# A projection stage written out by ticks of 24 matmuls, with convolution taps over about 1024 tokens

## The chip, the cores and the metric

The kernel runs on one core of one Trainium2 chip. The metric is the device time of one execution, in microseconds (us); of several runs the median counts. Engines are named as in the profile: PE is the matmul engine (PEld its weight loads), DVE the vector engine, ACT the scalar engine, POOL the GpSimd engine, SP the engine whose queue issues most DMA transfers. "L159" is line 159 of the kernel before.

## What is computed

An encoder layer is applied with the same weights to two requests, of 2048 and of 1024 tokens, all in float32. Cut to what matters:

```python
h = x @ w_in + b_in                       # 1024 -> 5632 features
glu_a, glu_b, conv_gate, q, k, v, attn_gate, m_conv, m_attn = split(h)
u = glu_a * sigmoid(glu_b)                # 512 channels
u = depthwise_conv(u, conv_dw) + conv_dw_b        # 31 taps along the tokens
u = silu(layer_norm(u)) * silu(conv_gate)
y_conv = u @ w_conv_proj + b_conv_proj
q, k = rope(q), rope(k)
o = rms_norm(differential_attention(q, k, v)) * silu(attn_gate)
merged = sigmoid(m_conv) * y_conv + sigmoid(m_attn) * (o @ w_attn_o)
y = layer_norm(alpha * x + merged @ w_out + b_out)
```

## The kernel before, in words

There are three stages. Stage A makes the projections `h`, finishes the convolution branch up to its SiLU, and spills everything to DRAM; stage B is the attention; stage C merges and projects out. Stages B and C are not touched, apart from comments.

**Precision.** A float32 matmul is made of three: an operand is split into a high part (ACT copies it in the matmul's rounded type) and a low part (the rest), and high x high, high x low and low x high are summed (`mm`, L287; `mm3`, L93). Every tile of weights is therefore split after it is loaded: high part on ACT (L126), low part on POOL (L127). Every tile of x is split by ACT (L283) and DVE (L284).

**Stage A.** The tokens come in three blocks of 1024 (two of the first request, one of the second). For each block, 22 chunks of 256 features are made in a fixed order (L211): sigmoid and linear halves of the GLU, then K, the convolution's gate, Q, the attention's gate, V, and the two sets of merge gates. A chunk is 96 matmuls of 128x512, in two halves of 48, each into a PSUM tile `psA` of two banks, of which there are three. V is made the other way round, with 128x256 matmuls, 192 to a chunk. When a half is complete it is evacuated (`evac`, L230; `evac_v`, L267):

- the GLU's second half and the gates by DVE with a PSUM input (L238, L243), after a sigmoid on ACT (L235, L242);
- Q and K by ACT (L254) and DVE (L255); four small DMAs swap quarter rows, POOL does two 128x1024 operations on the result (L259, L260), ACT rounds (L261), DVE subtracts (L262);
- V by four DVE additions (L272), an ACT copy (L273) and a DVE subtraction (L274);
- the merge gates by ACT alone (L248).

**The convolution.** It is done on DVE, one multiply-add per tap (L159). `conv_chunk` (L142) takes 512 tokens and all four channel tiles, two tiles at a time with their taps in turn, and then goes straight on, with the sums still in SBUF, to the layer norm over the channels: sums on POOL (L164 to L166), a split, a pair of matmuls with a matrix of ones into `psB` (L139), subtraction on DVE (L173), squares on ACT (L177) added on POOL (L179), a second pair of matmuls, square root on ACT (L186), reciprocal on DVE (L189), multiplications on DVE (L193, L196), sigmoid on ACT (L195), a product on POOL (L198), and the store (L199). It is a generator; `pump` (L204) takes so many steps of it after each half chunk, 6 in the first block and 11 in the others. The channels' last GLU chunk releases the convolution of those tokens whose neighbours are there: chunk 0 of 512 in the first block, chunks 1 to 3 in the second, both chunks of the second request in the third.

**What sets the order.** In stage A a planner does: it simulates the program with its own costs and gives each engine, and SP's queue of DMAs, the order that comes out. Only the first loads on SP are kept as written (L301). In stages B and C, PE, DVE, ACT and POOL run in program order inside a manual schedule (L589).

Of the kernel before, what the change touches and what calls it, by code (L numbers as in the profile page):

```python
# [11 lines left out]
F32 = mybir.dt.float32  # L12
F32R = mybir.dt.float32r
# [22 lines left out]
NE = 8  # L36
NST = NH * sum(LENS) // P
# [6 lines left out]
def encoder_kernel(ctx: ExitStack, tc: tile.TileContext, t: dict):  # L44
# [25 lines left out]
    # spills  # L70
    qd, kd, vd, sd, ud, cgd, agd, mcd, mad, ogd, ssqd, rrd = ([] for _ in range(12))
    for g, L in enumerate(LENS):
# [3 lines left out]
        sd.append([dram.tile([P, L], F32, name=f"sd{g}_{i}") for i in range(CT)])  # L76
        ud.append([dram.tile([P, L + 2 * HALO], F32, name=f"ud{g}_{i}") for i in range(CT)])
# [21 lines left out]
    # ---------------------------------------------------------------- phase A  # L99
    with ExitStack() as st:  # L100
        pool = lambda **k: st.enter_context(tc.tile_pool(reuse_waits="tile", **k))
        xp = pool(name="a_x", bufs=9)
        evm = pool(name="a_evm", bufs=3)
# [25 lines left out]
        def load_w(c):  # L129
            w = w_tiles()  # L130
            for i in (0, 4):
                split_w(w, i, i + 4, load_raw(t["w_in"][c, :, i:i + 4]))
            return w

        def total(x):
            """The mean over the channels, on every partition, of what the partitions hold of it."""
            ps = psB.tile([P, 512], F32, name="psB")
            for i, part in enumerate(split(cv, "tt", x, [P, 512], 1, nc.gpsimd)):
                nc.tensor.matmul(ps, ones_c, part, start=i == 0, stop=i == 1)  # L139
            return ps  # L140

        def conv_chunk(g, n):  # L142
            """The depthwise convolution of 512 tokens, its layer norm and SiLU, a step at a time."""
            t0 = n * 512
            acc = cv.tile([P, CT, 512], F32, name="acc")
            for c0 in range(0, CT, 2):
                us = []
                for c in (c0, c0 + 1):
                    u = cv.tile([P, 512 + 2 * HALO], F32, name="uc", bufs=3)
                    nc.sync.dma_start(u, ud[g][c][:, t0:t0 + 512 + 2 * HALO])  # L150
                    us.append(u)
                for k in range(TAPS):
                    for c in (c0, c0 + 1):
                        src = us[c - c0][:, k:k + 512]
                        if k == 0:
                            nc.vector.tensor_scalar(acc[:, c], src, dw_sb[:, c, 0:1], cvec[:, 0, c:c + 1],
                                                    op0=ALU.mult, op1=ALU.add)
                        else:
                            nc.vector.scalar_tensor_tensor(acc[:, c], src, dw_sb[:, c, k:k + 1], acc[:, c],  # L159
                                                           op0=ALU.mult, op1=ALU.add)  # L160
                        yield
            tmp = lambda: cv.tile([P, 512], F32, name="cvtmp", bufs=4)
            sm, sm2 = tmp(), tmp()
            nc.gpsimd.tensor_add(sm, acc[:, 0], acc[:, 1])  # L164
            nc.gpsimd.tensor_add(sm2, acc[:, 2], acc[:, 3])
            nc.gpsimd.tensor_add(sm, sm, sm2)  # L166
            for _ in range(4):
                yield
            mean = total(sm)
            for _ in range(3):  # L170
                yield
            for c in range(CT):
                nc.vector.tensor_sub(acc[:, c], acc[:, c], mean)  # L173
                yield
            for c in range(CT):
                s = cv.tile([P, 512], F32, name="cvsq", bufs=2)
                nc.scalar.activation(s, acc[:, c], AF.Square)  # L177
                if c:
                    nc.gpsimd.tensor_add(s, q2, s)  # L179
                q2 = s  # L180
                yield
            for _ in range(4):
                yield
            var = total(q2)
            sd_, rs = tmp(), tmp()
            nc.scalar.activation(sd_, var, AF.Sqrt, bias=eps_t)  # L186
            for _ in range(3):
                yield
            nc.vector.reciprocal(rs, sd_)  # L189
            for _ in range(5):  # L190
                yield
            for c in range(CT):
                nc.vector.tensor_mul(acc[:, c], acc[:, c], rs)  # L193
                sg = cv.tile([P, 512], F32, name="cvsq", bufs=2)
                nc.scalar.activation(sg, acc[:, c], AF.Sigmoid, bias=cvec[:, 2, c:c + 1], scale=cvec[:, 1, c:c + 1])  # L195
                nc.vector.tensor_scalar(acc[:, c], acc[:, c], cvec[:, 1, c:c + 1], cvec[:, 2, c:c + 1],  # L196
                                        op0=ALU.mult, op1=ALU.add)
                nc.gpsimd.tensor_mul(acc[:, c], acc[:, c], sg)  # L198
                nc.sync.dma_start(sd[g][c][:, t0:t0 + 512], acc[:, c])  # L199
                yield  # L200

        convs = []

        def pump(n):  # L204
            while n and convs:
                if next(convs[0], "end") == "end":
                    convs.pop(0)
                else:
                    n -= 1

        order = [GLU_B, GLU_A, GLU_B + 1, GLU_A + 1, K, CGATE, K + 1, CGATE + 1, Q, AGATE, Q + 1, AGATE + 1, V, V + 1]  # L211
# [18 lines left out]
        def evac(B, c, j, ps):  # L230
# [20 lines left out]
            else:  # L251
# [7 lines left out]
                nc.gpsimd.tensor_mul(sw, sw, B.sin)  # L259
                nc.gpsimd.tensor_add(qc, qc, sw)  # L260
                nc.scalar.activation(sw.bitcast(F32R), qc, AF.Copy)  # L261
                nc.vector.tensor_sub(qc, qc, sw)  # L262
                dst = qd if c < K else kd
                nc.sync.dma_start(dst[g][h][0, :, t0:t0 + TB], sw)
                nc.sync.dma_start(dst[g][h][1, :, t0:t0 + TB], qc)

        def evac_v(B, c, t4, ps):  # L267
            o = (c - V) * 256
            vt, vh = etile(), etile()
            vt4, vh4 = (x.rearrange("p (t e) -> p t e", e=256) for x in (vt, vh))  # L270
            for i in range(4):
                nc.vector.tensor_add(vt4[:, i], ps[:, i * 256:(i + 1) * 256], bv[:, o:o + 256])  # L272
            nc.scalar.activation(vh.bitcast(F32R), vt, AF.Copy)  # L273
            nc.vector.tensor_sub(vt, vt, vh)  # L274
            for i, x in enumerate((vh4, vt4)):
                r = B.b * 8 + t4 * 4
                nc.sync.dma_start(vd[B.g][i, r:r + 4, :, o:o + 256].rearrange("t p e -> p t e"), x)
# [9 lines left out]
        def mm(B, ps, w, j, k):  # L287
            """The k-tile's part of 128 features for the block's tokens."""
# [8 lines left out]
        # the function table, before the first inputs are there  # L297
# [3 lines left out]
        with tc.manual_schedule(engines={mybir.EngineType.SP}):  # L301
            for k in range(KT):
                if k % 4 == 0:
                    raw = ld.tile([P, TB], F32, name="raw")
# [531 lines left out]
```

## Time and profile before

| what | value |
|---|---|
| runs | 2822.12, 2823.57, 2825.48 us; median 2823.57 |
| span of the profiled execution, first to last instruction | 2816.1 us (its own time is not recorded apart from the span) |
| stage A, first to last matmul | 5.4 to 1548.0 us |
| its three blocks begin at | 5.4, 506.8 and 1009.0 us |
| PE, DVE, ACT, POOL busy, whole span | 96%, 65%, 38%, 53% |
| DMA | 364.89 MB, mean 130 GB/s |

How to read it: PE's busy time counts overlapping spans of pipelined matmuls, so a busy PE may still be waiting a little; the count of matmuls in a stretch says more. A table by stretches gives, for each engine, us busy and, in brackets, the number of instructions that began there; PEclk is the share of the full TensorE clock that was granted. A row of instructions gives line, engine, operation, output and inputs, shapes, count, then total us busy and mean ns of one, then the engine's idle time before them and who ended it.

### The profile page before, as it was taken

Reading aid. Unit: us, or ns where it says so; the run is one execution under the profiler, and the core shown is the slowest. Engines: PE = TensorE matmul, PEld = TensorE weight load, DVE = VectorE, ACT = ScalarE, POOL = GpSimd, SP = SyncE. Lnnn points to the kernel's source line nnn. Section 1 sums busy time; section 2 is a strip of 40 time slices with the busy share of each in tenths; the row PEclk is TensorE's granted clock in tenths of the full one; section 3 lists DMA queues with packets and bytes.
Section 4 is the critical chain, followed back from the end, with each engine's and each line's share of the span. In section 5 each row is a group of like instructions: output and inputs, shape, how many; then the busy total and the mean of one; then the engine's idle time right before and its main releaser. Section 6 shows DMA issues by size and latency. Waiting matters only on the chain. (4 is left out here: it accounts for less than half of the span.)

```text
span 2816.1 us, 36981 instructions
## 1 busy us (share of the span) xinstructions
PE 2709.3 (96%) x13818; PEld 2274.5 (81%) x13818; DVE 1843.1 (65%) x2564; ACT 1074.4 (38%) x1540; POOL 1478.5 (53%) x774
## 2 busy tenths in 40 slices
PE   9989999998999998979999999999999999999998
PEld 7868988887897877858878788888888877777777
DVE  4961110396387495994940888888888866667665
ACT  3122132212322222213121788878788822222121
POOL 3554232245535424546442899988888833333343
PEclk9999999999999999989999999999999999999999
DMA  6245323324443343334333332322234375566553
GB/s 194 71 152 179 126 105 112 143 72 158 157 142 119 108 138 104 105 127 156 105 116 112 109 85 88 85 69 70 69 94 116 104 253 190 182 207 200 181 162 119
DMA packets 194980, 364.89 MB, mean 130 GB/s; under 512 B 25088, under 2 KB 98288, under 8 KB 194800
## 3 DMA queue, kind: packets, MB, share of 16 engines
q1 hardware_dynamic: 193792, 362.22, 40.1%
q8 instruction: 109, 1.79, 0.3%
q14 instruction: 71, 0.58, 0.1%
q10 hardware_dynamic: 1008, 0.29, 0.1%
HBM read 242.67 MB, written 107.18 MB: 124 GB/s over the span
## 5 line engine op out<-in xcount | busy, mean ns | idle before, releaser
L127 POOL TENSOR_TENSOR wl<-raw,wh 128x1024 fp32r<-128x1024 f32 (+1 forms) x138 | 416.5, 3038 | 485.6 <-ACT wh L126 471.8
L291 PE MATMUL psA<-xh,wh 128*128 128x512 f32 x1920 | 600.6, 395 | 37.7 <-DVE ev L255 16.5
L159 DVE SCALAR_TENSOR_TENSOR acc<-uc,conv_dw,acc 128x512 f32<-128x512 f32 x720 | 608.5, 896 | 5.8
L291 PE MATMUL psA<-xl,wh 128*128 128x512 f32 x1920 | 598.6, 393 | 0.9 <-DVE xl L284 0.9
L291 PE MATMUL psA<-xh,wl 128*128 128x512 f32 x1920 | 597.7, 393 | 0.3 <-POOL wl L127 0.3
L291 PEld LDWEIGHTS psA<-xh,wh 128*128 128x128 f32 x1920 | 365.4, 191 | 116.9 <-DVE ev L255 17.8
L291 PEld LDWEIGHTS psA<-xl,wh 128*128 128x128 f32 x1920 | 365.4, 190 | 78.8 <-DVE xl L284 1.6
L291 PEld LDWEIGHTS psA<-xh,wl 128*128 128x128 f32 x1920 | 364.6, 190 | 77.6 <-POOL wl L127 1.0
L527 POOL TENSOR_TENSOR e<-e 128x2048 f32<-128x2048 f32 (+1 forms) x96 | 373.1, 3887 | 8.0
L505 PE MATMUL s<-km,qq 128*128 128x512 f32 x1280 | 352.3, 397 | 4.8 <-DVE e L507 4.4
L518 ACT ACTIVATE e<-e,mx 128x2048 f32<-128x2048 f32 (+1 forms) x192 | 329.5, 1716 | 1.2 <-DVE e L507 1.1
L507 DVE TENSOR_SCALAR_CACHE_REDUCE e<-s 128x1024 f32<-128x1024 f32 x192 | 233.4, 1216 | 77.1 <-PE s L505 75.7
L541 DVE TENSOR_TENSOR al<-tp,ah 128x512 fp32r<-128x512 f32 x320 | 220.1, 688 | 56.1 <-ACT ah L536 56.1
L505 PEld LDWEIGHTS s<-km,qq 128*128 128x128 f32 x1280 | 219.7, 189 | 41.3 <-DVE e L507 10.7
L126 ACT ACTIVATE wh<-raw 128x1024 fp32r<-128x1024 f32 (+1 forms) x138 | 134.0, 1012 | 285.0 <-PE psA L291 164.9
L536 ACT ACTIVATE ah<-tp 128x512 fp32r<-128x512 f32 x320 | 189.5, 593 | 98.7 <-PE tp L534 96.1
L90 POOL TENSOR_TENSOR zl<-zraw,zh 128x512 fp32r<-128x512 f32 x88 | 123.8, 1409 | 162.4 <-ACT zh L89 142.5
L95 PE MATMUL ops<-ah,vv 128*128 128x256 f32 x640 | 207.3, 324 | 0.2 <-ACT row L567 0.2
L534 PEld LDWEIGHTS tp<-ident,e 128*128 128x128 f32 x1280 | 158.6, 141 | 48.6 <-DVE al L541 3.7
L534 PE MATMUL tp<-ident,e 128*128 128x128 f32 x1280 | 193.3, 274 | 4.5 <-POOL e L527 3.0
L97 PE MATMUL ops<-al,vv 128*128 128x256 f32 x640 | 180.7, 282 | 0.7 <-DVE al L541 0.7
L96 PE MATMUL ops<-ah,vv 128*128 128x256 f32 x640 | 179.7, 281 | 0.0
(165 smaller groups left out, 4259.5 us busy)
## 6 DMA issues: line engine op xcount, KB each, us to landing
raw<-in_w_in SPq DMA_DIRECT2D x130, 512.0 KB
qq<-qd SPq DMA_DIRECT2D x384, 64.0 KB
zraw<-in_w_out SPq DMA_DIRECT2D x88, 256.0 KB
ev<-ev SPq DMA_DIRECT2D x96, 128.0 KB
kd<-ev SPq DMA_DIRECT2D x24, 512.0 KB
qd<-ev SPq DMA_DIRECT2D x24, 512.0 KB
vd<-ev SPq DMA_DIRECT2D x24, 512.0 KB
mcd<-evm SPq DMA_DIRECT2D x24, 512.0 KB
```

The lines of the kernel that those rows point to most:

```text
L95: nc.tensor.matmul(ps, ah, bh, start=first, stop=False)
L97: nc.tensor.matmul(ps, ah, bl, start=False, stop=last)
L127: nc.gpsimd.tensor_sub(lo, raw, hi.bitcast(F32))
L159: nc.vector.scalar_tensor_tensor(acc[:, c], src, dw_sb[:, c, k:k + 1], acc[:, c], op0=ALU.mult, op1=ALU.add)
L291: nc.tensor.matmul(ps[:, n * 512:(n + 1) * 512], w[a][:, k, j * P:(j + 1) * P], B.xs[k][x][:, n * 512:(n + 1) * 512], start=k == 0 and a = ...
L505: nc.tensor.matmul(s[:, n * 512:(n + 1) * 512], p.qt[2 * c + i][:, j * P:(j + 1) * P], p.km[c, hf][:, n * 512:(n + 1) * 512], start=i == 0 ...
L507: nc.vector.tensor_scalar(p.e[j, c][:, hf * 1024:(hf + 1) * 1024], s, -SCALE, mx[:, hf - 1:hf] if hf else None, op0=ALU.mult, op1=ALU.min, ...
L518: nc.scalar.activation(e, e, AF.Exp, bias=p.mx[j, c][:, nh - 1:nh], scale=-1.0, accum_out=sc)
L527: nc.gpsimd.tensor_add(e0, e0, e)
L534: nc.tensor.transpose(tp[:, i, j * P:(j + 1) * P], p.e[j, 0][:, kt * P:(kt + 1) * P], ident)
L536: nc.scalar.activation(ah, tp, AF.Copy)
L541: nc.vector.tensor_sub(al, tp, ah.bitcast(F32))
```

## The change

All of it is in stage A.

- **A manual order for four engines.** PE, DVE, ACT and POOL now run in program order. The program is cut into ticks of 24 matmuls (48 for V), four to a chunk. `later(n, f)` puts work off to the start of a later tick. SP's queue is still the planner's.
- **Evacuation** of a half comes one tick after its last matmul, the rotation of Q and K on POOL one tick after that, its rounding two ticks later still (`finish`); V's rounding a tick after its additions.
- **Weights** are loaded two chunks ahead and split in the first two ticks of the chunk before their own.
- **Convolution.** `conv_unit` takes one channel tile and all tokens of the block (1008, 1040 and 1024 of them), one tap after the other on the same sums, 2 taps per tick in the first two blocks and 3 in the third, and stores the raw sums to a new spill `sr`. A norm of 512 tokens (`norm`) later reads the four channel tiles back and runs by ticks; only one norm runs at a time, and it is begun when all four channel tiles of its block are done.
- **Buffers.** `ev` 5 to 7, `evm` 3 to 2; two `uc` and two `acc` of up to 1040 tokens (`uc` with 30 more); the scratch for dynamic DMA descriptors is set to 1024 bytes.
- **Lambda.** The small operations for lambda move to tick 5; the loads of small constants are issued on ACT behind the first splits.

By the program's bookkeeping, each block has 88 ticks. The GLU's last chunk ends with tick 16, and taps run from there: to tick 80 in the first two blocks, to tick 58 in the third. One norm begins at tick 81 of the first block; three in a row at tick 81 of the second block and at ticks 10 and 27 of the third; two at ticks 59 and 76 of the third. The last of these is in its second half when the last matmul of stage A is issued (tick 87).

The core of the diff:

```diff
-        evm = pool(name="a_evm", bufs=3)
+        evm = pool(name="a_evm", bufs=2)
...
-        ev = pool(name="a_ev", bufs=5)
+        ev = pool(name="a_ev", bufs=7)
...
+        tick, at = [0], defaultdict(list)
+        def later(n, f):
+            at[tick[0] + n].append(f)
+        def begin_tick():
+            for f in at.pop(tick[0], ()):
+                f()
+        def end_tick(taps):
+            pump(taps)
+            tick[0] += 1
...
+        def conv_unit(g, c, t0, t1):
+            n = t1 - t0
+            u = cv.tile([P, CONV_N + 2 * HALO], F32, name="uc", bufs=2)[:, :n + 2 * HALO]
+            nc.sync.dma_start(u, ud[g][c][:, t0:t1 + 2 * HALO])
+            acc = cv.tile([P, CONV_N], F32, name="acc", bufs=2)[:, :n]
+            yield
+            for k in range(TAPS):
+                src = u[:, k:k + n]
+                if k == 0:
+                    nc.vector.tensor_scalar(acc, src, dw_sb[:, c, 0:1], cvec[:, 0, c:c + 1], op0=ALU.mult, op1=ALU.add)
+                else:
+                    nc.vector.scalar_tensor_tensor(acc, src, dw_sb[:, c, k:k + 1], acc, op0=ALU.mult, op1=ALU.add)
+                yield
+            nc.sync.dma_start(sr[g][c][:, t0:t1], acc)
+
+        def norm(g, n):
+            r = slice(n * 512, (n + 1) * 512)
+            xs = [cv.tile([P, 512], F32, name="lx", bufs=CT) for _ in range(CT)]
+            for c in range(CT):
+                nc.sync.dma_start(xs[c], sr[g][c][:, r])
...
+            yield 3
+            parts = sum4(xs)
+            yield 3
+            m = mean(parts)
+            yield 1
+            sq = []
+            for x in xs:
+                nc.vector.tensor_sub(x, x, m)
+                sq.append(cv.tile([P, 512], F32, name="lq", bufs=CT))
+                nc.scalar.activation(sq[-1], x, AF.Square)
+            yield 1
+            parts = sum4(sq)
+            yield 3
+            m = mean(parts)
+            yield 1
...
+                def rotate():
+                    nc.gpsimd.tensor_mul(sw, sw, B.sin)
+                    nc.gpsimd.tensor_add(qc, qc, sw)
+                def finish():
+                    nc.scalar.activation(sw.bitcast(F32R), qc, AF.Copy)
+                    nc.vector.tensor_sub(qc, qc, sw)
...
+                later(1, rotate)
+                later(3, finish)
...
+        with tc.manual_schedule(engines={eng.PE, eng.DVE, eng.Activation, eng.Pool}):
...
+                rate = (2, 2, 3)[bi]
...
+                    for j in range(2):
+                        ps = psA.tile([P, TB], F32, name="psA")
+                        for i in range(2):
+                            step(2 * j + i)
+                            for k in range(4 * i, 4 * i + 4):
+                                mm(B, ps, w, j, k)
+                            if i == 1:
+                                later(1, lambda B=B, c=c, j=j, ps=ps: evac(B, c, j, ps))
+                            end_tick(rate)
...
+                if c == GLU_A + 1:
+                    t0, t1 = {(0, 0): (0, TB - 16), (0, 1): (TB - 16, 2 * TB), (1, 0): (0, TB)}[B.g, B.b]
+                    convs += [(B.g, i, t0, t1, conv_unit(B.g, i, t0, t1)) for i in range(CT)]
+            while at or convs or norms:
+                begin_tick()
+                end_tick(3)
...
-    nc = _bacc.Bacc("TRN2", target_bir_lowering=False, num_devices=1)
+    nc = _bacc.Bacc("TRN2", target_bir_lowering=False, num_devices=1, dynamic_dma_scratch_size=1024)
```

`sum4` makes three additions on POOL, a copy on ACT and a subtraction on POOL; `mean` makes two matmuls into `psB`; the rest of `norm` is as before, four channel tiles to a step. The first chunk of a block and the last one run both halves side by side over their four ticks, and in the last chunk the next block's x is loaded and split, two tiles to a tick, with no taps.

More of the change, by code (lines that the diff above doesn't have):

```diff
@@ L36 @@
 NE = 8
+CONV_N = TB + 16
 NST = NH * sum(LENS) // P
@@ L127, in split_w @@
             nc.gpsimd.tensor_sub(lo, raw, hi.bitcast(F32))
[L129 to L167, printed above, removed]
@@ L182, in conv_chunk @@
[L182 to L200, printed above, removed]
@@ L202, in encoder_kernel, with sum4, mean @@
-        convs = []
+                nc.sync.dma_start(xs[c], sr[g][c][:, r])
+            tmp = lambda: cv.tile([P, 512], F32, name="lt", bufs=2)
+            def sum4(parts):
+                a, b = tmp(), tmp()
+                nc.gpsimd.tensor_add(a, parts[0], parts[1])
+                nc.gpsimd.tensor_add(b, parts[2], parts[3])
+                nc.gpsimd.tensor_add(a, a, b)
+                return split(cv, "lm", a, [P, 512], 1, nc.gpsimd)
+            def mean(parts):
+                m = psB.tile([P, 512], F32, name="psB")
+                for i, part in enumerate(parts):
+                    nc.tensor.matmul(m, ones_c, part, start=i == 0, stop=i == 1)
+                return m
@@ new lines, in norm, with run_norms, start_norm @@
+            yield 2
+        convs, norms = [], []
+        def run_norms(it=None):
+            if it is None:
+                if not norms:
+                    return
+                it = norm(*norms.pop(0))
+            n = next(it, None)
+            if n is None:
+                normer[0] = False
+                start_norm()
+            else:
+                later(n, lambda: run_norms(it))
+        normer = [False]
+        def start_norm():
+            if norms and not normer[0]:
+                normer[0] = True
+                later(1, run_norms)
@@ L204, in pump @@
         def pump(n):
             while n and convs:
-                if next(convs[0], "end") == "end":
+                g, c, t0, t1, it = convs[0]
+                if next(it, "end") == "end":
                     convs.pop(0)
+                    if c == CT - 1:
+                        done[g] = t1
+                        while (normed[g] + 1) * 512 <= t1:
+                            norms.append((g, normed[g]))
+                            normed[g] += 1
+                        start_norm()
@@ L298, in encoder_kernel @@
         warm = cv.tile([P, 1], F32, name="warm")
-        nc.scalar.activation(warm, eps_t, AF.Sigmoid)
-        ws, xs = [w_tiles()], []
[L301 to L304, printed above, removed]
-                part = raw[:, k % 4 * 256:(k % 4 + 1) * 256]
-                nc.sync.dma_start(part, t["w_in"][order[0], :, k])
-                split_w(ws[0], k, k + 1, part)
-                parts = 1 if k else 2
-                xs.append(load_x(load_raw(t["xT"][0, :, k, :], parts), parts))
-            ws.append(load_w(order[1]))
-            B = Block(0)
-            B.xs = xs
```

227 lines of the change are left out of this document (131 added, 96 removed).

## The prediction

> **What bounds the kernel now.** I read the page first, then a table by stretches with the three blocks, two clean stretches and one crowded one, then PE's waits in stage A, then DVE and POOL in order of time.
>
> ```profile
> span 2816.1 us, 36981 instructions
> PE 2709.3 (96%) x13818; PEld 2274.5 (81%) x13818; DVE 1843.1 (65%) x2564; ACT 1074.4 (38%) x1540; POOL 1478.5 (53%) x774
> ```
>
> PE is the bound; no other engine is near it over the whole span. What stage A can gain is PE's lost time.
>
> ```profile
> core 0: us, PE busy (x) PEld busy (x) DVE busy (x) ACT busy (x) POOL busy (x), PEclk, DMA share, GB/s
> 5.40:506.80 501.40, 490.29 (x2308) 412.01 (x2309) 191.52 (x218) 124.67 (x131) 195.28 (x79) 0.99 0.41 137
> 506.80:1009.00 502.20, 489.74 (x2314) 411.21 (x2313) 317.14 (x385) 117.33 (x124) 229.19 (x84) 0.99 0.38 125
> 1009.00:1548.00 539.00, 497.46 (x2317) 415.56 (x2316) 354.02 (x406) 125.37 (x133) 227.63 (x94) 0.96 0.36 120
> 32.30:97.60 65.30, 65.30 (x289) 54.05 (x288) 43.41 (x55) 11.46 (x12) 32.95 (x7) 1.00 0.28 90
> 285.60:331.70 46.10, 46.10 (x386) 46.08 (x385) 9.62 (x16) 7.84 (x8) 10.52 (x4) 1.00 0.38 126
> 5.40:32.30 26.90, 26.03 (x96) 20.65 (x97) 12.50 (x25) 14.10 (x20) 10.34 (x9) 1.00 0.84 259
> 1121.40:1221.90 100.50, 93.22 (x399) 76.29 (x398) 94.63 (x103) 19.29 (x20) 50.24 (x14) 0.95 0.31 103
> ```
>
> The clean row 32.30 has 12 ticks, 288 matmuls, in 65.3 us: 0.2267 us each, 5.44 a tick. The V row has 384 in 46.1: 0.120 each. A block's 1920 and 384 thus need 435.3 + 46.1 = 481.4 us. The blocks lost 20.0, 20.8 and 57.6, together 98.4; the norms' 24 matmuls (5.4) are work, so **93 us are lost**. The first chunk, waiting for data (DMA share 0.84), is 5.1 of them: 26.9 against 21.8.
>
> ```profile
> PE psB L139 <- ACT tth L89: 28.5, 4, 13.6
> PE psA L291 <- DVE ev L255: 16.5, 3, 6.8
> PE psA L291 <- DVE ev L243: 11.9, 4, 5.0
> PE psA L291 <- ACT xh L283: 5.4, 1, 5.4
> ```
>
> PE waits for the norm's chain and for DVE to empty PSUM. The reason lies one step back:
>
> ```profile
> 75.36 19.30 DVE L159 SCALAR_TENSOR_TENSOR acc<-uc,conv_dw,acc 128x512 f32<-128x512 f32 x29
> 76.77 28.57 POOL L127 TENSOR_TENSOR wl<-raw,wh 128x1024 fp32r<-128x1024 f32 x4 [16.56 <-ACT wh L126]
> L127 POOL TENSOR_TENSOR wl<-raw,wh x138: 724/2408/22157, 4.1 to 1507.8; 128x1024 fp32r<-128x1024 f32 x130, 128x256 fp32r<-128x256 f32 x8
> ```
>
> While DVE runs taps of two channel tiles in turn, at 19.30/29 = 0.666 us, POOL's operation of 2.4 us stands still, up to 22.2 us. Work that follows POOL (weights, rotation, the norm's sums) is late in bursts.
>
> **The change part by part.** *Taps.* Each now follows on the same sums. One channel tile alone occurs in this trace too:
>
> ```profile
> 1418.75 23.59 DVE L159 SCALAR_TENSOR_TENSOR acc<-uc,conv_dw,acc 128x512 f32<-128x512 f32 x30
> 1242.73 16.07 DVE L159 SCALAR_TENSOR_TENSOR acc<-uc,conv_dw,acc 128x512 f32<-128x512 f32 x10
> 1243.36 2.40 POOL L259 TENSOR_TENSOR ev<-ev,sin 128x1024 f32<-128x1024 f32 x1 [14.91 <-DMA ev<-ev]
> 1245.84 2.72 POOL L260 TENSOR_TENSOR ev<-ev 128x1024 f32<-128x1024 f32 x1
> 1250.68 5.21 POOL L127 TENSOR_TENSOR wl<-raw,wh 128x1024 fp32r<-128x1024 f32 x2 [2.12 <-ACT wh L126]
> L711 DVE SCALAR_TENSOR_TENSOR xr<-xr,mv,ln_g_b x24: 1222/1274/2314, 2358.1 to 2810.2; 128x1024 f32<-128x1024 f32 x24
> ```
>
> Chained taps come at 23.59/30 = 0.786 us, and POOL gets in between them at once: four POOL operations run in 2.4 to 2.7 us, and ten taps take 16.07 instead of 7.9, so each costs DVE 8.2/4 = 2.05. A 1024-token tap is bounded by 2 x 0.666 = 1.33 and by L711's 1.274, the same operation at that size; with its hand-over I take 1.31. A block's 124 taps are 162 us, against 248 x 0.666 = 165: DVE's own work stays. What goes is the starving of POOL; what stays is that the two take turns.
>
> The price of taking turns is read from the crowded row, 1121.4 to 1221.9:
>
> ```profile
> L159 DVE SCALAR_TENSOR_TENSOR acc<-uc,conv_dw,acc 128x512 f32<-128x512 f32 x90 | 82.7, 986 | 0.0
> L255 DVE SCALAR_TENSOR_TENSOR ev<-psA,b_in_cols,cos 128x1024 f32<-128x1024 f32 x4 | 5.1, 1272 | 0.0
> L262 DVE TENSOR_TENSOR ev<-ev 128x1024 f32<-128x1024 f32 x4 | 4.9, 1217 | 5.9 <-ACT ev L261 5.9
> L243 DVE SCALAR_TENSOR_TENSOR ev<-psA,b_in_cols,ev 128x1024 f32<-128x1024 f32 x3 | 3.8, 1271 | 0.0
> L259 POOL TENSOR_TENSOR ev<-ev,sin 128x1024 f32<-128x1024 f32 x4 | 23.4, 5854 | 42.1 <-DVE acc L159 21.3 <-DMA ev<-ev 20.7
> L127 POOL TENSOR_TENSOR wl<-raw,wh 128x1024 fp32r<-128x1024 f32 x6 | 16.2, 2726 | 6.4 <-ACT wh L126 6.4
> L260 POOL TENSOR_TENSOR ev<-ev 128x1024 f32<-128x1024 f32 x4 | 10.6, 2645 | 0.3
> ```
>
> Undisturbed, DVE's work here is 90 x 0.666 + 5.1 + 4.9 + 3.8 = 73.7, and POOL's 14 x 2.4 = 33.6: 107.3 us of work took 100.5. So **the two together need 0.94 of the sum** of their times, where both have work all the time; PE, with 399 matmuls for 443, lost 10.
>
> The new program in 8 ticks of K, Q and gates (43.5 us of PE): 16 taps 21.0, four evacuations 5.1, two subtractions 2.4; POOL four weight splits and four rotations, 19.2. Sum 47.7, times 0.94 is 44.8: 1.3 behind, 5 over ticks 16 to 47. PE does not see it: a PSUM half is emptied one tick after it is full and needed again four ticks later, 21.8 us less the evacuation, about 20. After tick 56 DVE has taps alone, and a new wait on a late evacuation ends there. So in the first two blocks the 36 us lost behind the first chunk fall away.
>
> The third block has 3 taps a tick, and three norms in a row beside them until tick 44. Further durations:
>
> ```profile
> L189 DVE RECIPROCAL cvtmp<-cvtmp 128x512 f32<-128x512 f32 x6 | 20.1, 3353 | 83.6 <-ACT cvtmp L186 83.5
> L193 DVE TENSOR_TENSOR acc<-acc,cvtmp 128x512 f32<-128x512 f32 x24 | 15.0, 686 | 0.2
> L173 DVE TENSOR_TENSOR acc<-acc,psB 128x512 f32<-128x512 f32 x24 | 14.9, 682 | 51.5 <-PE psB L139 51.5
> L156 DVE TENSOR_SCALAR acc<-uc,conv_dw,conv_vecs x24: 534/547/2625, 54.5 to 1417.9; 128x512 f32<-128x512 f32 x24
> L179 POOL TENSOR_TENSOR cvsq<-cvsq 128x512 f32<-128x512 f32 x18 | 23.2, 1289 | 20.9 <-ACT cvsq L177 20.9
> ```
>
> Ticks 16 to 47 hold on DVE 93 taps (121.8), 16 evacuations of 1.27 (20.3), 8 subtractions of 1.22 (9.8), and of the norms 8 x 0.68, 2 x 3.35, 8 x 0.69 and 8 x 0.55 (22.1): 174.0. On POOL 32 operations of 2.4 and 20 of 1.29: 102.6. Sum 276.6; PE needs 174.1. By 0.94 it takes 260, 86 behind. Counted singly, 174.0 + 32 x 2.05 + 20 x 1.1 = 261.6, less what POOL does beside DVE operations that leave it alone, those with PSUM or a single tile as input (32.5 us; two thirds, since POOL isn't always waiting): 240, 66 behind. I take 76, and with a slack of 20 **PE waits 56 us in the third block**. Bounds: 0, if POOL fitted wholly beside DVE, since 174.0 alone is PE's time; 92, if nothing overlapped and the slack were half (276.6 - 174.1 - 10). In V's ticks 48 to 55, 39 of DVE and 9.6 of POOL stand against 46.1: the lag stays. Afterwards it drains.
>
> The Trainium skill, "SBUF — State Buffer", section "Who interferes with whom", states that DVE with two SBUF inputs and a reading GpSimd exclude each other, the later one blocking until the first is done, while DVE with one SBUF input doesn't contend. By that rule the 32.5 overlap whole, 276.6 - 32.5 = 244, and PE would wait 50. The trace agrees on the taking of turns (2.05 us a time), but not on issue order deciding: POOL's one operation waited through some 29 taps.
>
> *Smaller terms.* At both changes of block a norm's squares (ACT, behind four subtractions of 0.68 on DVE) stand ahead of the evacuation, and PE's second PSUM tile is wanted after 6 matmuls, 1.4 us; I estimate 3 us each, 6 (0 to 12). PE slowed after gaps: 4 (the loss in the third block has a clock of 0.96; where DVE sets the pace this costs nothing). The spill adds 12.6 MB to 364.9: 36 loads and stores on SP behind weights that are now a chunk earlier; with DMA shares under 0.41, nothing, and 5 if they crowd the x loads. The lambda work moves beside PE, nothing. The end:
>
> ```profile
> 1549.26 1.22 DVE L507 TENSOR_SCALAR_CACHE_REDUCE e<-s 128x1024 f32<-128x1024 f32 x1 [61.04 <-PE s L505]
> 1548.29 1.11 ACT L248 ACTIVATE evm<-psA,b_in_cols 128x1024 f32<-128x1024 f32 x1 [0.25 <-PE psA L291]
> ```
>
> Now DVE takes the first scores 1.3 us after stage A's last matmul, idle for 61 before. In the new order the last norm's reciprocal, products and scalings stand ahead, tied to four sigmoids behind two 1.11 evacuations on ACT: about 6, so 5 later (0 to 12).
>
> **Sum.** Lost after: 5.1 + 6 + 56 + 4 + 5 = 76, before 93: 17 gained. The sum is made against the span, 2816.1, which lies 7.5 under the median of the runs, 2823.6; I take those 7.5 as unchanged: 2807.
>
> **The rivals.** *Hidden turns (2761).* POOL finds its time in DVE's gaps: chained taps let it in at once, and it is busy only half of the crowded row. Then PE waits 10 instead of 56, gain 63. Against: that row still took 0.94 of the sum. *Strict turns (slower, 2843).* In the third block nothing overlaps, and the slack is not 20 but 10, because PE itself stands at the norm's second matmul pair, four ticks behind subtractions that are late on DVE, with three additions and a split on POOL between. PE waits 92 instead of 56: 36 more, 19 over the median. It is slower as soon as this wait passes 73. For it: psB is the largest of PE's waits already. Against: DVE's PSUM reads do overlap. *Order not fixed (2824).* SP's queue is still the planner's; where DVE is late, a store that waits holds the quarter swaps behind it, POOL stands, and the 17 are used up.
>
> **How the numbers follow.** Chances: forecast 0.48 (its own range 2789 to 2825, from waits of 46 to 66 and 8 either way in the small terms), hidden turns 0.20, strict turns 0.25, order not fixed 0.07. A measurement here can tell 0.2%, 5.6 us. Of the forecast's 0.48, 0.38 lie under 2818, 0.08 within, 0.02 above; of the last rival 0.04 within and 0.03 above. Faster 0.58, same 0.12, slower 0.30. The range reaches to both rivals: 2760 to 2846.
>
> **What would show it.** Right: in the first two blocks PE loses almost nothing behind the first chunk; no L127-like operation over 5 us; in the third block, ticks 16 to 47 take about 230 us for 174, with PE waiting for PSUM evacuations by DVE and for the norm's splits. Wrong: these ticks near 180 (hidden turns) or over 255 (strict turns), starving that goes on, or SP's swaps as what POOL waits for.

## The result, and the profile after

The changed kernel takes 2838.88 us (median of four runs, 2833.03 to 2843.72); the kernel before took 2822.85 beside it (2821.91 to 2825.48). The ratio is 1.0055, with an interval of 1.004 to 1.007: about 16 us slower, where 17 us faster were forecast. The profiled execution took 2833.03 us, the shortest of the four, and its span is 15.0 us longer than the one before.

The page of the changed kernel, span and busy times (from here on line numbers are those of the kernel whose rows are shown):

```profile
span 2831.1 us, 36651 instructions
PE 2710.6 (96%) x13818; PEld 2275.4 (80%) x13818; DVE 1925.9 (68%) x2192; ACT 1071.9 (38%) x1540; POOL 1438.1 (51%) x774
```

DVE does 372 instructions fewer and is busy 83 us more: the page alone says that its operations have become longer, not where this costs PE anything. That is read from the table by stretches. Its rows are the three blocks, a clean stretch (ticks 16 to 31 of the first block), the same ticks of the third block, its ticks 32 to 47, and the first four ticks of the second block.

```profile
4.89:494.05 489.16, 485.86 (x2306) 408.86 (x2307) 300.55 (x203) 111.76 (x115) 180.90 (x71) 1.00 0.45 145
494.05:988.70 494.65, 485.24 (x2310) 409.12 (x2309) 299.65 (x194) 111.95 (x113) 183.61 (x72) 0.99 0.41 135
988.70:1545.50 556.80, 504.83 (x2324) 420.47 (x2323) 339.37 (x234) 138.10 (x152) 241.22 (x110) 0.95 0.39 126
99.30:186.40 87.10, 87.10 (x386) 72.14 (x385) 77.16 (x41) 19.11 (x19) 46.20 (x16) 1.00 0.45 139
1087.30:1184.30 97.00, 91.39 (x388) 74.56 (x387) 90.69 (x57) 25.84 (x29) 54.90 (x22) 0.95 0.45 136
1184.30:1314.10 129.80, 98.33 (x390) 77.80 (x388) 123.40 (x73) 30.59 (x34) 70.95 (x30) 0.88 0.36 118
494.05:528.60 34.55, 25.14 (x99) 20.23 (x98) 5.83 (x7) 10.42 (x13) 9.75 (x6) 0.85 0.32 109
```

A block needs 481.4 us of matmuls, so the blocks lose 7.8, 13.3 and 75.4 us, 96.5 in all, where they lost 20.0, 20.8 and 57.6 before. The first two became 20 us cheaper, the third 18 us dearer. What the first two blocks gain, the third has eaten. Ticks 16 to 47 of that block (the two rows from 1087.30) take 97.0 + 129.8 = 226.8 us for 174. The first four ticks of the second block take 34.55 us for 21.8: that is the change of block, 12.8 us, and the one into the third block (988.7 to 1021.6) loses 32.9 - 21.8 = 11.1. So stage A ends at 1545.5 instead of 1548.0, hardly earlier.

PE's waits over the span, changed kernel:

```profile
PE psA L349 <- ACT evm L297: 18.4, 2, 9.4
PE s L601 <- DVE e L603: 16.4, 8, 7.7
PE psA L349 <- DVE ev L292: 11.0, 2, 7.7
PE psB L191 <- ACT lmh L91: 10.4, 3, 8.8
PE psA L349 <- POOL wl L144: 10.0, 3, 6.4
```

The largest wait of before, 28.5 us for the norm's split, is down to 10.4. The two new ones at the top lie elsewhere: two waits of some 9 us for an evacuation on ACT (the two changes of block), and the scores of stage B waiting for DVE. The latter is the seam between the stages, PE's matmuls of the scores and the first transpose:

```profile
1547.81 1.19 PE L601 MATMUL s<-km,qq 128*128 128x512 f32 x4 [1.25 <-ACT evm L297]
1553.72 3.78 PE L601 MATMUL s<-km,qq 128*128 128x512 f32 x8 [4.72 <-DVE e L603]
1565.20 4.72 PE L601 MATMUL s<-km,qq 128*128 128x512 f32 x12 [7.70 <-DVE e L603]
1581.79 0.27 PE L630 MATMUL tp<-ident,e 128*128 128x128 f32 x1
```

From stage A's last matmul to the first transpose it took 1569.2 - 1548.0 = 21.2 us before; now it takes 1581.8 - 1545.5 = 36.3, so 15.1 us are lost here. With 2.5 us won in stage A and 2.4 lost after the first transpose, the span is 15.0 longer. (From the first transpose to the end, the kernels of this study take between 1245.0 and 1249.3 us, though no edit touches that part; a difference of 2 us in one profile says nothing.)

What the same stretch of time shows on DVE:

```profile
1541.01 3.35 DVE L211 RECIPROCAL lt<-lt 128x512 f32<-128x512 f32 x1 [25.99 <-ACT lt L210]
1549.19 3.33 DVE L219 TENSOR_SCALAR lx<-lx,conv_vecs 128x512 f32<-128x512 f32 x3 [0.15 <-ACT lq L216]
1552.45 1.21 DVE L603 TENSOR_SCALAR_CACHE_REDUCE e<-s 128x1024 f32<-128x1024 f32 x1
1563.91 1.22 DVE L603 TENSOR_SCALAR_CACHE_REDUCE e<-s 128x1024 f32<-128x1024 f32 x1 [8.83 <-DMA sd<-lx]
```

The last norm's reciprocal begins at 1541.0, after 26 us in which DVE waited for ACT's square root: it is the norm's own chain that is late, not a busy DVE. The norm holds DVE until 1552.5, then the first scores are taken. The third one waits another 8.83 us, and the releaser is a store of the norm, `sd<-lx`. The tile `e` of stage B and the norm's tiles `lx` have nothing else to do with each other, so it must stand in memory that these had, and may be written only when they have been stored. POOL has finished the first of the four tiles at 1550.4 and the last at 1554.9, but SP issues the first store at 1556.93, behind loads of the next stage:

```profile
1552.17 2.76 SPq L674 DMA_DIRECT2D wraw<-in_w_conv_proj  x1
1554.97 1.86 SPq L569 DMA_DIRECT2D vv<-vd  x2
1556.93 3.48 SPq L221 DMA_DIRECT2D sd<-lx  x4
```

And the change of block, on ACT (the times answer to the last row of the table above):

```profile
495.17 1.06 ACT L341 ACTIVATE xh<-raw 128x1024 fp32r<-128x1024 f32 x1 [1.39 <-DMA raw<-in_xT]
498.56 1.06 ACT L341 ACTIVATE xh<-raw 128x1024 fp32r<-128x1024 f32 x1 [2.34 <-DMA raw<-in_xT]
501.51 2.42 ACT L203 ACTIVATE lq<-lx 128x512 f32<-128x512 f32 x4 [1.89 <-DVE lx L201]
503.84 2.10 ACT L297 ACTIVATE evm<-psA,b_in_cols 128x1024 f32<-128x1024 f32 x2
504.98 1.22 PE L349 MATMUL psA<-xh,wh 128*128 128x512 f32 x2 [9.41 <-ACT evm L297]
```

ACT could have emptied the last chunk's PSUM at about 495.5. In program order there stand ahead of it the last x tile of the next block, which waits for its load until 498.56, and the norm's four squares, which wait for DVE until 501.51. The evacuations begin at 503.84, and PE, which found a free tile for its first matmuls only, goes on at 504.98.

That last load is late for want of a buffer. Pool `ld` has four, and the weights of the next chunk hold two of them. SP issues the load 0.02 us after DVE has subtracted an earlier x tile (493.81 + 1.23), and ACT starts on the new tile 3.5 us after that:

```profile
493.81 1.23 DVE L342 TENSOR_TENSOR xl<-raw,xh 128x1024 fp32r<-128x1024 f32 x1 [3.19 <-ACT xh L341]
495.06 0.33 SPq L131 DMA_DIRECT2D raw<-in_xT  x1
```

Last, POOL and the taps over the whole span:

```profile
L144 POOL TENSOR_TENSOR wl<-raw,wh x138: 723/2413/3418, 3.7 to 1505.7; 128x1024 fp32r<-128x1024 f32 x130, 128x256 fp32r<-128x256 f32 x8
L169 DVE SCALAR_TENSOR_TENSOR acc<-uc,conv_dw,acc x360: 1186/1300/3435, 103.2 to 1403.2; 128x1008 f32<-128x1008 f32 x60, 128x1040 f32<-128x1040 f32 x60, 128x1024 f32<-128x1024 f32 x60
```

The longest split of weights on POOL is 3.4 us; it was 22.2. The middle tap is 1.30 us (1.31 was taken), but the longest is 3.4: a tap now shares its time with POOL, instead of POOL standing still. By groups, in ticks 32 to 47 of the third block:

```profile
L169 DVE SCALAR_TENSOR_TENSOR acc<-uc,conv_dw,acc 128x1024 f32<-128x1024 f32 x47 | 98.3, 2092 | 1.2
L144 POOL TENSOR_TENSOR wl<-raw,wh 128x1024 fp32r<-128x1024 f32 x8 | 25.8, 3235 | 26.7 <-ACT wh L143 26.7
L311 POOL TENSOR_TENSOR ev<-ev 128x1024 f32<-128x1024 f32 x5 | 16.3, 3265 | 7.7 <-DVE ev L304 7.5
```

A tap takes 2.09 us there in the mean, 0.79 over the middle one; over 47 taps that is 37 us, and the stretch loses 42.8 (129.8 - 87.0).

### The profile page after: what moved, and what is told of

It is laid out like the page before. It is cut to its first block, busy times and chain, and to the rows that moved or that the text cites. A ratio compares the mean times of both kernels' runs of the same rounds, so it can differ in the third digit from the quotient of the medians.

```text
span 2831.1 us, 36651 instructions
## 1 busy us (share of the span) xinstructions
PE 2710.6 (96%) x13818; PEld 2275.4 (80%) x13818; DVE 1925.9 (68%) x2192; ACT 1071.9 (38%) x1540; POOL 1438.1 (51%) x774
## 3 DMA queue, kind: packets, MB, share of 16 engines
q10 hardware_dynamic: 1008, 0.29, 0.1%
## 4 chain that ended last, share of the span: by engine, by line
PE 75%; DVE 12%; DMA 6%; issue 4%; ACT 2%; POOL 1%; SPq 1%; DVEq 0%; ACTq 0%; POOLq 0%
PE psA L349 35%; PE s L601 10%; DVE acc L169 6%; PE tp L630 5%; PE y L97 3%; PE y L98 3%; PE y L99 3%; PE ops L97 3%; PE ops L99 3%; PE ops L98 3%; PE z L99 2%; PE z L97 2%; PE z L98 2%; DMA raw<-in_xT 1%; DMA x<-sd 1%
## 5 line engine op out<-in xcount | busy, mean ns | idle before, releaser
L144 POOL TENSOR_TENSOR wl<-raw,wh 128x1024 fp32r<-128x1024 f32 (+1 forms) x138 | 368.7, 2685 | 721.8 <-ACT wh L143 713.3
L169 DVE SCALAR_TENSOR_TENSOR acc<-uc,conv_dw,acc 128x1008 f32<-128x1008 f32 (+2 forms) x360 | 667.0, 1853 | 9.5
L601 PE MATMUL s<-km,qq 128*128 128x512 f32 x1280 | 354.5, 400 | 17.7 <-DVE e L603 16.4
L614 ACT ACTIVATE e<-e,mx 128x2048 f32<-128x2048 f32 (+1 forms) x192 | 329.3, 1715 | 15.0 <-DVE e L603 13.3
```

The source lines that it names most:

```text
L144: nc.gpsimd.tensor_sub(lo, raw, hi.bitcast(F32))
L169: nc.vector.scalar_tensor_tensor(acc, src, dw_sb[:, c, k:k + 1], acc, op0=ALU.mult, op1=ALU.add)
L601: nc.tensor.matmul(s[:, n * 512:(n + 1) * 512], p.qt[2 * c + i][:, j * P:(j + 1) * P], p.km[c, hf][:, n * 512:(n + 1) * 512], start=i == 0 ...
L614: nc.scalar.activation(e, e, AF.Exp, bias=p.mx[j, c][:, nh - 1:nh], scale=-1.0, accum_out=sc)
```

## The experiments

The theory after this reading: three causes that add up. DVE and POOL take turns, and the third block asks for more of both than its chunks last (60 us in ticks 16 to 55); at the changes of block the evacuation stands behind other work on ACT (24); at the seam the last norm and then its stores hold the scores (15). The rival: time is merely moved about, and what one edit frees, another wait takes. Each ratio is to the kernel before, run on the same chip with it (2817.5 to 2820.3 us there); the changed kernel stands at 1.0055. "Loss" is time over that of the matmuls.

**Shorter waits in the last norms.**

```diff
+            brisk = g == 1
...
-            yield 3
+            yield 2 if brisk else 3
...
-            yield 2
+            yield 1 if brisk else 2
```

> The two norms of the second request take 13 ticks each instead of 17 and so end four ticks before the last matmul of stage A; nothing else changes. Theory: the 15 us that are lost at the change to stage B (first transpose 21 us after the last projection before, 36 us after) come from the last norm, whose operations stand ahead of the first scores on DVE and whose tiles are stored late while stage B wants their memory. Then the run is about 15 us shorter than the changed kernel, 2824, and DVE's first scores follow within 2 us. Rival: the start of stage B waits for its own loads; then no gain, 2839.

2825.14 us, ratio 1.0025 (1.0015 to 1.0034). The seam is back at 21.7 us (1558.5 to 1580.2), 14.6 less. But ticks 56 to 72 of the third block lose 14.7 us where they lost 2.8, and PE's waits say for what:

```profile
PE psB L192 <- ACT lmh L91: 20.7, 3, 10.2
```

The norm's mean is a pair of matmuls in PE's own program order. With shorter waits it is due while DVE still lags from the ticks before: the last tap ends at 1403.6, its sums go out and come back by DMA, POOL adds them from 1413.9 (1413.8 in the changed kernel), and PE stands from 1407.0 to 1417.2. By the ratios 8.5 us are won, where 15 were expected. The seam was what the theory said; here the rival has a part too, but only as long as the third block is overfull.

**Evacuations first at the change of block.** The last chunk's evacuations are put ahead of what waits in that tick, and the last x tile behind them.

```diff
-                                later(1, lambda B=B, c=c, j=j, ps=pss[j]: evac(B, c, j, ps))
+                                at[tick[0] + 1].insert(j, lambda B=B, c=c, j=j, ps=pss[j]: evac(B, c, j, ps))
+                            if raws:
+                                at[tick[0] + 1].insert(2, next_x)
...
-                        next_x()
```

> At the two changes of block the PSUM evacuations are put ahead of the norm's squares and of the last x tile on ACT. Theory: the 24 us lost there (12.8 and 11.1 in the first four ticks of a block) come from ACT's order alone; PE's second PSUM tile then comes free about 1 us after the last matmul, the gaps of 9.8 and 9.4 us go, and the run is about 18 us shorter, 2821. Rival: the x tiles themselves land late (ACT waited 40 us for them in all), and PE meets that a little later; then at most 5 us shorter, 2834.

2811.7 us, ratio 0.9977 (0.9966 to 0.9988). The changes lose 4.2 and 2.0 us instead of 12.8 and 11.1 (the first four ticks of the second and third block, 21.8 of matmuls each):

```profile
495.12:521.10 25.98, 24.17 (x100) 19.49 (x99) 6.07 (x7) 10.83 (x14) 9.79 (x6) 0.93 0.44 146
981.10:1004.90 23.80, 22.56 (x100) 18.36 (x99) 5.29 (x7) 10.52 (x13) 9.79 (x6) 1.00 0.50 154
```

By the ratios 22 us are won, 17.7 of them here, so the rival (5 at most) falls. This edit alone makes the changed kernel slightly faster than the one before, by some 6 us.

**Only past the norm.** The same without the lines for `next_x`: evacuations ahead of the norm's step, still behind the last x tile.

> Only half of the reordering of the second experiment: the last chunk's evacuations go ahead of the norm's step (four subtractions on DVE, four squares on ACT), but stay behind the last x tile of the next block. In the changed kernel's trace the last x tile ends on ACT at 499.6 us, the squares at 503.9, and the evacuations follow; PE wanted them at about 495.5. Theory 1 (each of the two costs its own time in ACT's queue): about 4.3 us of each change of block go, its loss falls from 12.8 and 11.1 to about 8 each, the run is 8 us shorter than the changed kernel, ratio to the kernel before about 1.0025, and the rest of the gain of the second experiment belongs to the late x tile. Theory 2 (the norm's step was all of it): the changes lose about 6 in all as in the second experiment, ratio about 0.998. Theory 3 (the late x tile was all of it): ratio stays about 1.0055.

2818.91 us, ratio 1.0003 (0.9991 to 1.0016). The changes lose 7.9 and 8.4 us. The ACT rows of the first of them:

```profile
498.55 1.06 ACT L341 ACTIVATE xh<-raw 128x1024 fp32r<-128x1024 f32 x1 [2.49 <-DMA raw<-in_xT]
499.51 2.10 ACT L297 ACTIVATE evm<-psA,b_in_cols 128x1024 f32<-128x1024 f32 x2
501.51 2.41 ACT L203 ACTIVATE lq<-lx 128x512 f32<-128x512 f32 x4
```

So of the 24 us, 7.6 belonged to the norm's step and a further 10.1 to the x tile that was loaded late, as the first theory had it. Its ratio of 1.0025 was not met: by the ratios 15 us are gone. Of the rest the profile shows 2.4 us at the seam and 3.2 after it, where nothing was changed, so the split rests on the profiles, not on the times.

**Without the rotation on POOL.** For the second request, the two POOL operations that rotate K and Q are left out.

```diff
                 def rotate():
+                    if B.bi == 2:
+                        return
```

> Leaves out POOL's two operations of the rotation of K and Q, for the second request alone (16 operations of 2.4 us in the third block's ticks 16 to 47); DVE's work stays as it is. Theory: the third block's loss comes from DVE and POOL taking turns; without these, 16 x 2.05 to 2.4, 33 to 38 us, fall away, ticks 16 to 47 take about 192 instead of 227, the run 2803. Rival: DVE's own work and the chain of the norm set the pace there, POOL runs beside it; then the run stays within 8 us, 2832 to 2839.

2805.9 us, ratio 0.9956 (0.9941 to 0.9971), some 28 us less. Ticks 16 to 47 of the third block take 89.3 + 113.1 = 202.4 us instead of 226.8, and V's ticks 46.1 instead of 53.6. The theory had 192 for the former; the rival (within 8 us) falls. Not one DVE instruction was taken away, and yet the taps of ticks 32 to 47 became shorter, 1671 ns instead of 2092:

```profile
L169 DVE SCALAR_TENSOR_TENSOR acc<-uc,conv_dw,acc 128x1024 f32<-128x1024 f32 x49 | 81.9, 1671 | 1.2
```

POOL's work is paid for in DVE's time: that is the taking of turns, shown by removing one side of it. Sixteen operations less gave 31.9 us in ticks 16 to 55 (24.4 and 7.5), 2.0 each, the 2.05 that the prediction read from ten taps in the trace of before.

**Taps over two channel tiles in turn,** as before, at the new length.

```diff
+            for k in range(TAPS):
+                for i, u, acc in zip((c - 1, c), us, accs):
...
+                    yield
```

> The taps go over two channel tiles in turn, as before the change, with all else as changed (four buffers for their inputs). Theory: a tap then no longer waits for the one just before it, the taps come closer (1.2 instead of 1.31 us) and POOL stands still behind whole runs of them, up to 15 us and more at a time; the first two blocks lose again 5 to 15 us each and the third more than now: 2845 to 2880. Rival: the order of the taps doesn't matter to POOL, and DVE's shorter taps help the third block: 2825 to 2832.

2891.5 us, ratio 1.0253 (1.0235 to 1.0272). The starving of POOL is back, and worse than before; POOL's splits and PE's two longest waits:

```profile
L144 POOL TENSOR_TENSOR wl<-raw,wh x138: 725/2409/43120, 3.7 to 1555.7; 128x1024 fp32r<-128x1024 f32 x130, 128x256 fp32r<-128x256 f32 x8
```

```profile
PE psA L352 <- POOL wl L144: 54.6, 5, 22.7
PE s L604 <- DMA qq<-qd: 29.5, 1, 29.5
```

It costs more than expected, and at another place than in the kernel before, whose first two blocks lost 14.0 and 11.4 us in ticks 16 to 31: now they lose 22.9 and 25.4 us in ticks 56 to 72, beside the merge gates, which ACT alone empties, so that DVE has taps and nothing else. Two splits stood there, for 41.5 and 43.1 us; no other operation of POOL in stage A took over 3.5. Where DVE also empties PSUM (ticks 16 to 47), POOL gets its turns in between, and in the first two blocks those ticks lose nothing. The starts of the taps show the difference: beside the longest split the 33 taps began every 1.21 us at 1.29 each, so that each began before the last one had ended; in the changed kernel they begin every 1.34 us at 1.30, and where a POOL operation comes between, after 3.36. The third block's ticks 16 to 72 lose about the same as in the changed kernel (58.6 and 63.0). The seam is 15.8 us longer: the first scores wait for loads of Q, which SP issues from 1617.3 on, behind the norm's stores and the loads of K; in the changed kernel they were issued from 1408.1 on. Why the planner put them there stays open. So taps that each need the last one's result are worth about 48 us in the new order, in places where the kernel has nothing else on DVE.

**The taps spread otherwise.** The same operations at other ticks: the units of channel tiles 0 and 1 begin one chunk earlier, and the rates are 2 (3 under V in the third block) and 2, 3 or 4 beside the merge gates.

```diff
-                rate = (2, 2, 3)[bi]
+                rate = 3 if c < CGATE else (2, 2, 3)[bi] if c in (V, V + 1) else (2, 3, 4)[bi] if c >= MCONV else 2
...
-                if c == GLU_A + 1:
+                if c in (GLU_A, GLU_A + 1):
...
-                    convs += [(B.g, i, t0, t1, conv_unit(B.g, i, t0, t1)) for i in range(CT)]
+                    convs += [(B.g, i, t0, t1, conv_unit(B.g, i, t0, t1))
+                              for i in (2 * (c - GLU_A), 2 * (c - GLU_A) + 1)]
```

> The taps are only spread otherwise over a block: the units of channel tiles 0 and 1 begin one chunk earlier, two units per tick (three in the last block under V) stand beside most chunks and two, three or four per tick beside the merge-gate chunks, so that fewer of the twelve seconds of taps stand in ticks 16 to 47, where in the third block the rotation, the evacuations and the taps want DVE and POOL at once. Theory 1 (DVE and POOL take turns, and the third block's loss is the surplus of the sum of their times over the time of the chunks): ticks 16 to 47 of the third block fall from 226.8 us to about 180, V's loss of 7.5 goes, the run is 45 to 50 us shorter than the changed kernel, ratio to the kernel before about 0.988. Theory 2 (the loss there is the chain from a matmul's end through its own evacuation and is not a matter of load): the run stays within 10 us of the changed kernel, ratio 1.002 to 1.009. The norms of the third block end a few ticks later than now, so the seam is no shorter than its 36 us.

2769.35 us, ratio 0.9829 (0.9816 to 0.9843), some 64 us less than the changed kernel. The third block's ticks 16 to 31 and 32 to 47:

```profile
1086.40:1174.40 88.00, 88.00 (x389) 72.83 (x389) 80.13 (x47) 27.33 (x30) 57.61 (x23) 1.00 0.42 141
1174.40:1265.30 90.90, 88.98 (x386) 73.16 (x386) 86.76 (x48) 21.49 (x21) 51.77 (x18) 0.98 0.52 159
```

178.9 us instead of 226.8, and V loses nothing. Nothing was made shorter or left out; DVE has 48 instructions in the second stretch, where it had 73. Its 33 taps still take 1.92 us each, so the turns are still taken. They only fit now. The theory's number was right (180) and the rival's (within 10 us) fell. The seam stays at 34.2 us. Of the 60.9 us between the two spans, ticks 16 to 47 give 47.9, V 7.5, the ticks behind it 1.8, the first two blocks 4.0 and the seam 2.1, while the change into the third block costs 3.2 more. The expectation's two terms, 47 and 7.5, were met; its total of 45 to 50 lies under their sum.

**With the evacuations first as well.** The spread and the order of the second experiment together.

> The other spread of the taps and the evacuations ahead at the change of block, with the norm's waits as in the changed kernel (three ticks). Theory 1 (the short waits in the norms were worth only the seam): the seam stays at about 34 us instead of 21, everything before it is as in the version with all three edits, so the run is about 13 us longer than that one, ratio to the kernel before about 0.978. Theory 2 (the short waits cost PE time in stage A, which this kernel gets back): less than 8 us longer, ratio under 0.976.

2762.25 us, ratio 0.9796 (0.9779 to 0.9813). The change into the second block loses 1.9 us, but the one into the third 9.6, and PE's row there is

```profile
989.94 1.22 PE L350 MATMUL psA<-xh,wh 128*128 128x512 f32 x2 [7.16 <-ACT evm L298]
```

again behind an x tile that its load brought late. The order on ACT removes the queueing behind the last x tile only; when the tile before it is late too, the wait returns. Here it can be followed further back:

```profile
965.34 9.16 SPq L131 DMA_DIRECT2D raw<-in_w_in  x2
968.69 0.63 ACT L91 ACTIVATE lmh<-lt 128x512 fp32r<-128x512 f32 x1 [6.42 <-POOL lt L186]
```

The second of these two loads of weights stands ahead of the next load of x in SP's queue and waits 8.4 us for a buffer that DVE's subtraction of an x tile frees. DVE waits for ACT's copy of that tile, and ACT has the norm's rounding ahead of it, which waited 6.42 us for POOL. No run changes this alone. The seam is 34.9 us, as the first theory had it.

**All three: spread, evacuations first, two ticks instead of three in every norm.**

> The other spread of the taps, the evacuations ahead of the norm's step at each change of block, and the shorter waits (two ticks) in every norm, together. Theory 1 (three causes that add: turns in the third block, the evacuation's place in ACT's queue at the changes, the last norm at the seam): lost PE time in the third block's ticks 16 to 55 falls from 60 to about 5, at the changes of block from 24 to about 6, and the seam from 36 to about 21: 85 to 90 us shorter than the changed kernel, ratio to the kernel before about 0.975. Theory 2 (the short waits bring back the wait of PE on the norm's mean, as they did in ticks 56 to 72 where DVE lagged): 10 to 15 us of that come back, ratio about 0.980. Theory 3 (the causes do not add, one pool of DVE time that only moves): ratio above 0.99.

2739.36 us, ratio 0.9734 (0.9716 to 0.9752): 75 us faster than the kernel before, 91 faster than the changed one. The three blocks:

```profile
5.00:494.20 489.20, 485.82 (x2309) 408.23 (x2310) 308.92 (x216) 120.97 (x127) 189.85 (x79) 1.00 0.44 147
494.20:979.50 485.30, 483.47 (x2313) 407.92 (x2312) 302.56 (x199) 117.52 (x121) 193.02 (x80) 1.00 0.42 139
979.50:1466.20 486.70, 484.49 (x2317) 408.67 (x2316) 317.15 (x223) 129.30 (x137) 220.12 (x98) 1.00 0.44 142
```

They lose 7.8, 3.9 and 5.3 us of 481.4, the granted clock is 1.00 throughout, and the seam is 21.3 us (1466.2 to 1487.5). The three causes do add, as the first theory had it: in the profiles stage A gives 79.4 and the seam 15.0 of the 97.0 us between the spans. The short waits, which cost 12 us where the third block was overfull, cost nothing here. Against the version without them it is 0.0062 by the ratios, 17 us, of which 13.6 are the seam; the two profiles lie 26.8 apart, and of the rest 7.1 is the late x tile of that version's profile.

**The last stores on another queue.**

```diff
-                nc.sync.dma_start(sd[g][c][:, r], x)
+                (nc.scalar if (g, n) == (1, 1) else nc.sync).dma_start(sd[g][c][:, r], x)
```

> The four stores of the last norm are issued on ACT's queue instead of SP's, where they stand behind the loads of the next stage. Theory 1 (the first part of the scores waits for the memory of the norm's tiles, which comes free when these stores have landed): DVE's 8.8 us wait for the store at the seam shrinks to under 4, the seam goes from 36.3 to about 32, the run is 4 to 5 us shorter than the changed kernel, ratio to the kernel before about 1.004. Theory 2 (the scores would have been late anyway through the exponentials and the transposes, or ACT is held by issuing the stores): seam within 1 us of 36.3 and ratio about 1.0055.

2830.51 us, ratio 1.0041 (1.0028 to 1.0054). DVE's wait at the seam:

```profile
1563.65 1.22 DVE L603 TENSOR_SCALAR_CACHE_REDUCE e<-s 128x1024 f32<-128x1024 f32 x1 [4.92 <-DMA sd<-lx]
```

8.83 became 4.92 (under 4 was expected), the seam 36.3 became 32.9. So the queue made up some 4 us of that wait; the rest is the stores themselves, which follow the norm's end. The ratios' intervals overlap, so the run's time alone wouldn't show it; the row does.

## Why the prediction was wrong

*What held.* The first two blocks lose almost nothing behind the first chunk except where they change. No split on POOL takes over 3.4 us. In the third block ticks 16 to 47 took 226.8 us, forecast about 230, and PE's loss from tick 16 to tick 71 was 9.9 + 42.8 + 7.5 + 2.8 = 63.0, forecast 56 of waiting and 4 of slow clock. Both "hidden turns" (ticks near 180) and "strict turns" (over 255) fell. That the measured 2838.88 us lies near the 2843 of "strict turns" is chance: that rival put its 36 us into the third block, and 28 us of the error lie elsewhere. Of "order not fixed" little is left, though no run moved the swaps: in ticks 16 to 55 of the third block POOL waits 14.0 us for them, 8.4 at the longest, and 76.3 us for ACT's high parts of the weights. The run without the rotation showed the turns directly, and their price. The size of the 56 is in part luck, for it stands on the middle of two estimates 20 us apart (66 and 86 behind), and the 32.5 us of the lower one leave out the eight scalings (8 x 0.55 = 4.4), which have a single tile as input too; with them it would be 63.

*What failed.* The step is "Smaller terms", in two of its numbers. Changes of block were put at 6 us (bounds 0 and 12) and took 23.9; the end was put at 5 (0 to 12) and took 15.1. Together that is 28 us, and the sum was off by 32.0 (2831.1 against 2816.1 - 17). The other 4 are the 3 us in the third block and the odd microseconds after the seam.

*Changes of block.* The prediction saw the norm's squares ahead of the evacuation on ACT, at 3 us each; they cost 3.8 each (the experiment that goes past the norm only). It didn't see the last x tile, which stands ahead of both in the same program order and itself waits for a load: 10.1 us at the two changes. The sentence "with DMA shares under 0.41, nothing, and 5 if they crowd the x loads" looked at how busy the DMA engines are, but the load was late because SP could issue it only when a buffer came free (495.06). The estimate and its bound of 12 name work of ACT and DVE alone, and an engine that takes its work in order and waits for a DMA is not bounded by that.

*The end.* That DVE would take the first scores about 5 us later was right: 1552.45 is 7.0 after the last matmul, where it was 1.3. The other 8.8 us came from a wait that no row of before could show, a tile of the next stage in the memory of the norm's tiles. The prediction took the end to be done when the norm's arithmetic was done, but its stores are part of what the next stage waits for, and they too stand in a queue.

*The third block.* The forecast priced this stretch nearly right and then took it for a given. Its own count could have told that it was not: the sum of DVE's and POOL's work in ticks 16 to 47, 276.6 us against 174, stands beside ticks after 56 with taps alone or none. Spreading the taps otherwise took 64 us off the run without removing one instruction.

The Trainium skill, "SBUF — State Buffer", section "Who interferes with whom", has a DVE instruction with two SBUF inputs and a GpSimd instruction that reads SBUF exclude each other, the later one blocking until the first is done. The runs agree on the exclusion (2.0 us of DVE's time for each POOL operation taken out) and not on the order: with taps in turn over two tiles a POOL operation stood for 43.1 us, through 33 taps that began after it. (What the Trainium skill says there of operations with one SBUF input excepts those in a two-port mode; the prediction left that out, and no run here tests it.)

## What to carry to other kernels

Before costing a program order by durations, follow each in-order queue at every seam and ask of every instruction ahead of the urgent one what it waits for, loads and stores included: two small terms of this sum, 6 and 5 us, held 28 us of its error of 32. When two engines take turns, count the sum of both in each stretch and move work to stretches that have room; the averages of a page (DVE 68%, POOL 51%) say nothing of it. An edit that frees one wait is worth its full size only when the stretch that it touches isn't overfull: in one version the short norm waits won 14.6 us at the seam and lost 11.9 before it, in the other they won 13.6 and lost nothing.

## What the runs showed that was not expected

- With taps in turn POOL starved only where DVE had taps alone: 41.5 and 43.1 us beside the merge gates, under 3.5 us for every operation in ticks in which DVE also empties PSUM.
- The granted clock was lower where PE had gaps: 0.88 in the stretch that lost 42.8 us, 0.85 in the four ticks after the first change of block, 1.00 over all three blocks in the version with all three edits. After the gap of 9.41 us pairs of matmuls start every 0.86 us, where 0.45 is usual (changed kernel, PE):

```profile
506.00 1.05 PE L349 MATMUL psA<-xl,wh 128*128 128x512 f32 x2
506.86 1.05 PE L349 MATMUL psA<-xh,wl 128*128 128x512 f32 x2
507.71 1.05 PE L349 MATMUL psA<-xh,wh 128*128 128x512 f32 x2
```

- From the first transpose on, where no edit was made, the kernels differ by up to 4.3 us between profiles (1245.0 to 1249.3). And the last x tiles come late by different amounts at the two changes of one run: with evacuations first and the taps spread, one change lost 1.9 us and the other 9.6. The rows beside that experiment show what the second waited for; loads of weights stand among those of x in SP's order, and no run moved only these.
